# The 31-step inverse of the triangular blocks on GpSimd instead of VectorE, in a GLA + RWKV-7 layer on one Trainium2 core

## The chip, the cores and the metric

One core of a Trainium2 chip runs the whole layer. The metric is device time in microseconds (us), the median over several runs of the kernel; less is better. Beside the times there is one profiled execution with its trace. Engine names in the profile: PE is TensorE (PEld its weight loads), DVE is VectorE, ACT is ScalarE, POOL is GpSimd, SP is SyncE, which issues all DMAs of this kernel.

## What is computed

One inference step of a hybrid decoder layer, in float32, for a prompt of 1024 rows and 8 single-token samples, width 1024. A projection `w_in` (1024 to 9360 columns) feeds two branches and two gates:

```python
p = einsum('btd,dn->btn', x, w_in)                  # GLA, RWKV-7 and gate columns
S = diag(a_t) S + k_t^T v_t ;  o_t = q_t S          # GLA, 4 heads of 128 x 256
S = S (diag(w_t) - kk_t^T (kk_t * a_t)) + v_t^T k_t # RWKV-7, 16 heads of 64 x 64
y_t = S r_t
m = sigmoid(gate_a) * (o_gla @ w_up_gla) + sigmoid(gate_b) * (o_rwkv @ w_up_rwkv)
y = layernorm(2**0.25 * x + m @ w_out)
```

The outputs are `y`, the new states of both branches and the last projected row. The RWKV-7 recurrence is the part that matters here. In chunks of 64 tokens it becomes matrix products, if for each chunk and head the inverse of a unit triangular 64 x 64 matrix is at hand.

## The kernel before

**Stages.** The prompt is worked in two passes of 512 tokens (`PASS`; the samples ride with the first). In both passes TensorE computes `w_in` by rows of 128 columns, every product as three fp32r products of high and low halves (`blocks`, lines 670 to 705). While these run, each finished group of rows feeds a stream of its own: four GLA heads (`gla_head`) and eight pairs of RWKV heads (`pair`) in each pass, so 16 pairs in all. Then come the two up projections, and last `w_out` with the layer norm.

**A pair** runs `front`, `back`, `turn`, `chain` and `norm`. `front` (line 1060) computes decays and keys, then for its eight chunks the products `big<-az,wide`, masked into the tile `gg` (lines 1125 to 1130). The diagonal 32 x 32 blocks of these are written to DRAM (`LD`) and read back (`wide<-LD`, lines 1137 to 1145) so that 128 partitions hold 128 entries of work: 32 blocks, each four times, eight columns of the inverse for each partition. Lines 1147 to 1152 form the inverse by substitution: 31 steps, each a `tensor_mul` into the tile `Xt` and a `tensor_add` of it into the tile `X`. Every one of the 62 instructions reads what the one ahead of it wrote. Step j handles `ni = j // 4 + 1` rows of `w = 31 - j` elements, 8 to 76 elements for each partition. Then `X` goes to DRAM (`XD`) and back in another layout (`XT<-XD`), and `back` (line 1179) begins: `Xt<-XT` transposes on VectorE, then the products `big<-Xt,L` on TensorE which complete the 64 x 64 inverse. `chain` runs the eight chunks of the recurrence one after the other; pair p's chain waits for that of pair p - 1. There is one `X`, one `Xt`, one `L1`, and buffers for two pairs.

**What sets the order.** All engines run instructions in the order in which the program gives them, and a planner in the kernel (class `Order`, lines 239 to 402) writes that order. Each stream yields one instruction at a time; `run` takes the one with the smallest key (its start by the planner's own clock, less a priority). The start comes from `start`: when the engine is free, when the inputs are ready (plus a hop between engines, 0.13 for the same engine), and, for VectorE and GpSimd instructions that `shared` names (two SBUF inputs and the like), when the other of the two engines has left the shared port. `price` (lines 145 to 174) gives each instruction's cost. Instructions made through `self.E` may go to VectorE or GpSimd, whichever ends first by that clock, those through `self.C` to ScalarE or VectorE. So a change of engine or of price moves instructions everywhere. Every instruction is recorded through one helper, so that the profile shows line 217 for all; the tiles tell them apart.

The lines that the diff touches are 171 (in `price`) and 1150 and 1152 (in `front`).

## Time and profile before

| | |
|---|---|
| median of 3 runs | 1603.45 us (1600.87 to 1605.56) |
| profiled execution | 1597.82 us, span 1596.0 us |
| PE busy / PEld busy | 1550.1 us (97%) / 1371.0 us (86%) |
| DVE busy | 1282.5 us (80%), 3351 instructions |
| ACT busy | 855.9 us (54%) |
| POOL busy | 123.5 us (8%), 218 instructions |
| granted TensorE clock | 0.997 |

How to read it: busy time is the sum of an engine's instructions, the span runs from the first to the last instruction. Matmuls are pipelined and their ends are modelled, so PE's busy time also covers short holes between them. A group's row in the profile gives the engine, the operation, the tile written and the tiles read, the shape of output and input, the count, then busy time in us and the mean of one in ns, then the idle time of the engine ahead of them and what ended it. In the views of stretches, each engine has its busy time with the number of instructions in brackets.

### The profile page before, as it was taken

What the parts mean: (1) busy time and instruction counts of PE and PEld (TensorE: products, weight loads), DVE (VectorE), ACT (ScalarE), POOL (GpSimd) and SP (SyncE); (2) the same over time, 40 slices, a digit from 0 to 9 for tenths busy, and PEclk for the clock granted to TensorE, in tenths of its full rate; (3) what the DMA queues carried; (4) which work ended last, traced back from release to release, by engine and by line L of the source; (5) the groups of instructions that cost most, each with busy time, mean ns of one, the idle gap of its engine ahead of it and who ended that gap; (6) DMA issues with size and microseconds to landing.
All of it is one profiled execution on the core that took longest, in us unless ns stands there. A gap on an engine that the chain in (4) does not pass through costs nothing.

```text
span 1596.0 us, 29099 instructions
## 1 busy us (share of the span) xinstructions
PE 1550.1 (97%) x9874; PEld 1371.0 (86%) x9874; DVE 1282.5 (80%) x3351; ACT 855.9 (54%) x2032; POOL 123.5 (8%) x218
## 2 busy tenths in 40 slices
PE   8999999999999999999999999999999999999998
PEld 6999999999999998787888777878777889988786
DVE  6697889878989798779788997899877786756565
ACT  5564666566657665553654464445454646544210
POOL 2011001100000011001101120011001000000000
PEclk9999999999999999999999999999999999999999
DMA  9767776676757765755465546544665467797332
GB/s 308 245 233 221 231 232 224 204 260 222 232 188 250 246 219 184 213 162 172 144 194 161 168 119 212 168 152 134 204 174 144 161 211 255 255 300 251 128 117 82
DMA packets 206641, 318.42 MB, mean 200 GB/s; under 512 B 87076, under 2 KB 102573, under 8 KB 206493
## 3 DMA queue, kind: packets, MB, share of 16 engines
q1 hardware_dynamic: 206492, 316.56, 62.6%
q8 instruction: 79, 1.29, 0.3%
q14 instruction: 70, 0.57, 0.1%
HBM read 196.82 MB, written 118.61 MB: 198 GB/s over the span
## 4 chain that ended last, share of the span: by engine, by line
PE 60%; DVE 23%; DMA 6%; SPq 4%; issue 4%; ACT 3%; POOL 0%; DVEq 0%; POOLq 0%; ACTq 0%
PE proj L217 30%; PE big L217 19%; DVE row L217 8%; PE pY L217 7%; PE pch L217 4%; SPq L217 4%; DVE Xt L217 3%; DVE X L217 3%; DVE wide L217 2%; DVE wpart L217 2%; DMA wide<-LD 1%; DVE az L217 1%; DMA wraw<-w_in 1%; ACT row L217 1%; DVE pair L217 1%
## 5 line engine op out<-in xcount | busy, mean ns | idle before, releaser
L217 PE MATMUL proj<-xh,wpart 128*128 128x256 f32 (+2 forms) x3744 | 915.5, 328 | 2.4 <-DMA wpart<-w 2.0
L217 PEld LDWEIGHTS proj<-xh,wpart 128*128 128x128 f32 x3744 | 624.2, 189 | 52.3 <-issue 5.1
L217 PE MATMUL proj<-xl,wpart 128*128 128x264 f32 (+2 forms) x1872 | 611.6, 327 | 0.9 <-DVE xl L217 0.7
L217 PEld LDWEIGHTS proj<-xl,wpart 128*128 128x128 f32 x1872 | 353.3, 189 | 25.4 <-issue 1.7
L217 ACT CAST wpart<-wraw 128x512 fp32r<-128x512 f32 x210 | 130.3, 623 | 113.7 <-PE proj L217 44.0
L217 DVE TENSOR_TENSOR wpart<-wraw,wpart 128x512 fp32r<-128x512 f32 x207 | 142.3, 689 | 38.1 <-ACT wpart L217 37.3
L217 DVE TENSOR_TENSOR row<-row 128x512 f32<-128x512 f32 (+10 forms) x302 | 164.0, 549 | 7.3 <-ACT row L217 2.4
L217 ACT ACTIVATE row<-row 128x512 f32<-128x512 f32 (+5 forms) x229 | 139.1, 611 | 36.0 <-DVE row L217 25.2
L217 DVE TENSOR_TENSOR Xt<-X,wide 128x60 f32<-128x60 f32 (+24 forms) x496 | 108.7, 219 | 17.9 <-DMA wide<-LD 6.8
L217 DVE TENSOR_TENSOR X<-X,Xt 128x60 f32<-128x60 f32 (+24 forms) x496 | 109.0, 220 | 12.3 <-DVE Xt L217 0.5
L217 ACT ACTIVATE s0p<-wide,pc 64x64 f32<-64x64 f32 x256 | 88.0, 344 | 46.7 <-DVE wide L217 41.0
L217 POOL TENSOR_TENSOR row<-row 128x256 f32<-128x256 f32 (+5 forms) x67 | 67.2, 1005 | 575.8 <-DVE row L217 238.6
L217 ACT ACTIVATE row<-proj,omu 128x256 f32<-128x256 f32 (+1 forms) x99 | 54.1, 547 | 98.6 <-PE proj L217 98.4
L217 PE MATMUL big<-row 128*128 128x128 f32 (+3 forms) x520 | 96.4, 287 | 9.4 <-DVE Xt L217 4.0
L217 PEld LDWEIGHTS big<-row 128*128 128x128 f32 (+1 forms) x520 | 74.8, 187 | 20.0 <-ACT row L217 11.3
L384 ACT ACT_TABLE_LOAD x66 | 84.7, 1283 | 1.1
L217 DVE SCALAR_TENSOR_TENSOR wide<-pch,pc,s0p 64x64 f32<-64x64 f32 x224 | 63.2, 282 | 22.7 <-PE pch L217 17.4
L217 DVE SCALAR_TENSOR_TENSOR row<-proj,pv,row 128x255 f32<-128x255 f32 (+1 forms) x99 | 56.2, 568 | 26.6 <-ACT tail L217 17.5
L217 PE MATMUL big<-xh,wpart 128*128 128x512 f32 (+2 forms) x304 | 74.8, 329 | 0.0
L217 ACT COPY row<-big 128x128 f32<-128x128 f32 (+5 forms) x134 | 38.5, 317 | 64.8 <-PE big L217 56.5
L217 PE MATMUL big<-az,wide 128*128 128x256 f32 x256 | 66.4, 384 | 0.4 <-DVE row L217 0.2
L217 PE MATMUL big<-part,headsr 128*128 128x512 f32 x128 | 55.7, 440 | 7.3 <-ACT part L217 3.4
(240 smaller groups left out, 2506.9 us busy)
## 6 DMA issues: line engine op xcount, KB each, us to landing
w<-wpart SPq DMA_DIRECT2D x146, 512.0 KB
wpart<-w SPq DMA_DIRECT2D x146, 512.0 KB
wraw<-w_in SPq DMA_DIRECT2D x146, 256.0 KB
wide<-LD SPq DMA_DIRECT2D x64, 128.0 KB
wraw<-w_up_gla SPq DMA_DIRECT2D x32, 256.0 KB
wraw<-w_up_rwkv SPq DMA_DIRECT2D x32, 256.0 KB
sg<-row SPq DMA_DIRECT2D x16, 260.0 KB
row<-sg SPq DMA_DIRECT2D x16, 260.0 KB
```

What stands on the lines that cost most here:

```text
L217: ways.append((eng, lambda call=call: call(out, *args, **kw), price(eng, name, out, args, ins)))
L384: self.nc.scalar.preload_act_table_set(self.table)
```

## The change

Both instructions of each of the 31 steps are issued on GpSimd (`self.G`) instead of VectorE (`V`). Nothing else of the pair is altered: the memsets of `X` stay with `self.E`, the DMAs on SP. A second edit is in the planner: a `copy_predicated` on VectorE is priced at 480 elements a microsecond instead of 960. It issues no other instruction, but takes part in the order.

```diff
@@ price @@
         scalars = sum(x.free_size() == 1 for x in ins[1:]) if name in ("scalar_tensor_tensor", "tensor_scalar") else 0
-        return 0.068 + wide / 960 + 0.06 * scalars
+        return 0.068 + wide / (480 if name == "copy_predicated" else 960) + 0.06 * scalars
     if name in ("tensor_scalar", "memset"):
         return 0.08 + n / 760
     return 0.1 + n / (300 if name == "tensor_copy" else 456)
@@ front @@
         for j in range(31):
             w, ni = 31 - j, j // 4 + 1
             tv = tm[:, :ni * w].rearrange("p (s t) -> p s t", t=w)
-            yield V.tensor_mul(tv, X[:, 0:ni, j:j + 1].to_broadcast([P, ni, w]),
+            yield self.G.tensor_mul(tv, X[:, 0:ni, j:j + 1].to_broadcast([P, ni, w]),
                                L[:, j:j + 1, j + 1:].to_broadcast([P, ni, w]))
-            yield V.tensor_add(X[:, 0:ni, j + 1:], X[:, 0:ni, j + 1:], tv)
+            yield self.G.tensor_add(X[:, 0:ni, j + 1:], X[:, 0:ni, j + 1:], tv)
         self.free(tm)
```

## The prediction, made before the changed kernel was run

> **What bounds the kernel now.** First the page: busy shares, the chain of work that ended last, and the two groups that the change moves (busy us, mean ns of one, idle time ahead of them).

> ```profile
> PE 1550.1 (97%) x9874; PEld 1371.0 (86%) x9874; DVE 1282.5 (80%) x3351; ACT 855.9 (54%) x2032; POOL 123.5 (8%) x218
> ...
> PE 60%; DVE 23%; DMA 6%; SPq 4%; issue 4%; ACT 3%; POOL 0%; DVEq 0%; POOLq 0%; ACTq 0%
> ...
> L217 DVE TENSOR_TENSOR Xt<-X,wide 128x60 f32<-128x60 f32 (+24 forms) x496 | 108.7, 219 | 17.9 <-DMA wide<-LD 6.8
> L217 DVE TENSOR_TENSOR X<-X,Xt 128x60 f32<-128x60 f32 (+24 forms) x496 | 109.0, 220 | 12.3 <-DVE Xt L217 0.5
> ```

> TensorE is the bound: 97% busy, 60% of the chain. VectorE is second with 23% of the chain; GpSimd is empty. All TensorE idle time together is 1596.0 - 1550.1 = 46 us, the most that taking other engines out of its way is likely to win. Next, one stretch that holds the projection with the pairs, then the 16 stretches in which an inverse is formed (first `Xt` to last `X`; first, last and sum of 16), and the tile X alone in the same stretches. Columns: us, then each engine's busy time.

> ```profile
> 100.00:1300.00 1200.00, 1169.82 (x7552) 1039.79 (x7551) 1028.99 (x2855) 692.62 (x1692) 111.65 (x197) 1.00 0.62 193
> ```

> ```profile
> 77.00:114.40 37.40, 36.91 (x300) 36.34 (x299) 36.42 (x126) 20.30 (x49) 4.24 (x6) 1.00 0.73 253
> ...
> 1271.90:1298.10 26.20, 23.46 (x140) 20.84 (x139) 23.82 (x84) 13.90 (x25) 0.00 (x0) 0.93 0.79 275
> sum 475.40, PE 464.35 PEld 418.26 DVE 435.75 ACT 238.17 POOL 24.40; mean PE 29.02 PEld 26.14 DVE 27.23 ACT 14.89 POOL 1.53
> ```

> ```profile
> sum 475.40, DVE 217.47 POOL 0.00; mean DVE 13.59 POOL 0.00
> ```

> The order of the columns is PE, PEld, DVE, ACT, POOL. An inverse now takes 475.4 / 16 = 29.7 us, of which its own instructions are 13.6; the rest is other VectorE work between its steps. VectorE is 92% busy there (435.75 of 475.4) and 86% in the whole stage (1029 of 1200). TensorE loses only 11 us in these stretches: the projection covers the inverse. Third, what TensorE's queue waits for (sum, times, longest):

> ```profile
> PEld big L217 <- ACT row L217: 14.7, 20, 2.2
> PEld big L217 <- issue: 10.4, 16, 4.5
> PEld pch L217 <- DVE rh L217: 9.2, 20, 1.5
> PEld proj L217 <- issue: 6.8, 9, 0.9
> PEld big L217 <- DVE part L217: 5.7, 13, 1.3
> PEld big L217 <- ACT part L217: 5.1, 5, 2.7
> PEld big L217 <- DVE Xt L217: 3.9, 7, 1.3
> ```

> Many short waits. Over all 33 rows of that view, of which these are the first by size, those ended by VectorE sum to 31 us, those by ScalarE to 26. They are what a lighter VectorE can shorten.

> **What goes from VectorE.** 496 x 0.219 + 496 x 0.220 = 217.7 us. In the built program VectorE has 1026 instructions fewer (992 of the inverse, 34 others that the planner places elsewhere); POOL has 992 more and 22 besides. Table loads on ScalarE fall from 66 to 56:

> ```profile
> L384 ACT ACT_TABLE_LOAD x66 | 84.7, 1283 | 1.1
> ```

> ```profile
> L217 DVE COPY_PREDICATED row<-lev,big 128x256 f32<-128x256 uint8 x40 | 29.5, 737 | 1.1 <-PE big L217 0.8
> ```

> That is 10 x 1.28 = 12.8 us of ScalarE, which at 54% has room: I count nothing for it (bounds 0 to -5 us). The new price of `copy_predicated`, 0.068 + 256/480 = 0.60, is nearer to 0.737 than the old 0.33; it only makes the order truer, and I count nothing for it either (-5 to +5 us, as any reshuffling).

> **What a step costs on POOL.** The trace has no POOL instruction of 8 to 76 elements in these forms, so it is bounded by neighbours: groups by form, then one tile's minimum / median / maximum, then the timeline (start, us) and a stretch with two instructions back to back.

> ```profile
> L217 POOL TENSOR_TENSOR row<-row 128x256 f32<-128x256 f32 x29 | 24.3, 839 | 277.8 <-DVE row L217 96.3 <-PE big L217 96.0 <-DVE Xt L217 50.6
> L217 POOL TENSOR_TENSOR row<-row 128x8 f32<-128x8 f32 x4 | 1.1, 283 | 5.0 <-DVE row L217 4.9
> L217 POOL TENSOR_TENSOR row<-row 128x32 f32<-128x32 f32 x1 | 0.2, 240 | 10.4 <-issue 10.4
> L217 DVE TENSOR_TENSOR wpart<-wraw,wpart 128x512 fp32r<-128x512 f32 x207 | 142.3, 689 | 38.1 <-ACT wpart L217 37.3
> ```

> ```profile
> L217 POOL TENSOR_TENSOR row<-row x67: 203/1007/1925, 92.8 to 1258.4; 128x256 f32<-128x256 f32 x29, 128x512 f32<-128x512 f32 x22, 128x520 f32<-128x520 f32 x6, 128x8 f32<-128x8 f32 x4
> L217 POOL TENSOR_TENSOR part<-row,part x12: 1284/1327/1808, 268.7 to 1205.2; 128x512 fp32r<-128x512 f32 x12
> ```

> ```profile
> 263.80 0.63 POOL L217 TENSOR_TENSOR row<-row 128x256 f32<-128x256 f32 x1 [10.47 <-DVE row L217]
> ```

> ```profile
> 459.25:460.17 0.92, 0.84 (x2) 1.00 0.19 76
> ```

> The 31 products have sum(ni x w) = 1560 elements, 50.3 on the mean. Between 32 elements (0.240) and 256 undisturbed (0.63) the slope is 1.74 ns, so 50.3 elements take 0.272 us; 0.08 us lies between two neighbours (0.92 - 0.84). A step of 0.352 x 62 = **21.8 us** for an inverse that nothing disturbs. From below: 0.203 + 0.08, 17.5 us. From above: the mean rows, waits included, 0.283 at 8 and 0.839 at 256 elements, give 0.376 + 0.08, 28.3 us; and POOL against VectorE at 512 elements, 1284 / 689 = 1.86, times 0.2195 gives 0.409 + 0.08, 30.3 us. I take 21.8, since 32 elements is by far the nearest row.

> **The port.** POOL and VectorE hold each other up. VectorE alone, and POOL in the same stretch; then a POOL instruction behind a VectorE one:

> ```profile
> 494.29 0.22 DVE L217 TENSOR_TENSOR Xt<-X,wide 128x54 f32<-128x54 f32 x1
> 494.43 0.48 DVE L217 SCALAR_TENSOR_TENSOR row<-row 128x256 f32<-128x256 f32 x1
> 494.82 1.30 DVE L217 TENSOR_TENSOR X<-X,Xt 128x54 f32<-128x54 f32 x1
> ```

> ```profile
> 494.56 1.49 POOL L217 TENSOR_TENSOR part<-row,part 128x512 fp32r<-128x512 f32 x1 [32.36 <-ACT part L217]
> ```

> ```profile
> 758.84 0.68 DVE L217 TENSOR_TENSOR part<-row,part 128x512 fp32r<-128x512 f32 x1
> ...
> 759.07 0.52 POOL L217 TENSOR_TENSOR row<-row 128x4 f32<-128x4 f32 x1 [0.96 <-DVE row L217]
> ```

> `X` of 54 elements took 1.30 instead of 0.22 and ended with POOL's; POOL's 4 elements took 0.52 instead of 0.203, to 0.07 after VectorE's end. The other VectorE work in the stretches is 435.75 - 217.47 = 218.3 us in 475.4, a share of 0.46; I put half of it at instructions with two SBUF inputs (estimate from the groups; 0.3 to 0.7). In 25 us that is 5.8 us, some 8 instructions of 0.69, each holding a POOL step for about 0.5: **4.2 us** (2.5 to 6). VectorE in turn loses at most 8 x 0.27 x 16 = 35 us of its 218. The inverse then takes 21.8 + 4.2 = **26.0 us**, less than today's 29.7.

> **What of it shows.** TensorE executes in order: the products `big<-Xt,L` wait for the inverse, and everything behind them (projection, chain) waits with them. The planner has moved them: in the built program 292 TensorE instructions stand between the last `big<-az,wide` and the first `big<-Xt,L` of a pair on the mean, 320 before (368 for 429 in the first pass, 217 for 211 in the second). At 1200 us for 7552 records, 0.159 us (an f32 product leaves two records, so this is the least), 28 fewer are 4.4 us less cover, so an inverse of 29.7 - 4.4 = 25.3 us is just in time. Lateness: 0.7 us x 16 = **+11 us**. POOL's queue is in order too: behind a step stand low halves (`part`, `wpart`) and `row` products for TensorE. Most have had tens of us of idle time ahead of them, so a step of 0.35 matters little; cost nothing, bound +5 us. The four `XD<-X` DMAs stay in SP's queue and start when the last add ends, on another engine; no cost.

> Relief: VectorE in the stage falls from 1029 to about 1029 - 204 + 35 = 860 of 1200 us (15 of the 16 inverses), 86% to 72%; its idle share doubles, so I halve the 31 us of waits that it ends, and take a quarter off ScalarE's 26, which often stand behind VectorE: **-22 us** (0 to -46).

> Sum: 1597.8 + 11 - 22 = 1587 against the profiled execution, which lies 0.35% under the runs' median; on the median's scale **1592 us**, 0.7% faster.

> **Rivals.**

> (A) The step is priced by the mean rows, 0.456 us, and an inverse takes 28.3 us: 3.0 us late each, +48 - 22 = +26, **1629 us**, slower. It decides in the same place, the first `big<-Xt,L`, from an inverse of about 26.7 us on, where 16 latenesses of 1.4 eat the 22 us. For it: the means hold the port's waits that a busy VectorE causes. Against: 203, 240 and 0.63 are undisturbed.

> (B) POOL keeps its factor of 1.86 over VectorE on short instructions: 30.3 + 4.2 = 34.5 us, 9.2 late, 16 x 9.2 - 22 = +125, about **1728 us**. Against it: the fixed part would have to be 0.3 us, and 203 ns rows exist. [...]

> (C) TensorE is the bound anyway and lateness and relief cancel: 1598 to 1608, **1603 us**. For it: TensorE's 97%. That the move does not take place at all is excluded by the built order.

> **How the numbers follow.** Forecast 0.50, A 0.24, B 0.12, C 0.14. About 0.3% (4.8 us) is what a measurement here can tell from no change. The forecast's own spread, 1570 to 1600, lies almost wholly under 1598.6: faster 0.50. C gives same 0.14; A and B slower 0.36. Low end 1565: nearly all 46 us of TensorE's idle time gone. High end 1650: A with the larger port share (6 us for 4.2, 16 x 1.8 = 29 us, partly). Outside lie B and some 0.07 of tails.

> **What would show it.** Right: POOL busy from 123 to about 420 us (992 x 0.272 + 147), VectorE about 1050 to 1100, inverses near 26 us, waits of PEld for `rh`, `part` and `row` shrinking, that for `Xt` about 10 us more. Wrong: POOL's `X` rows at 0.35 us or more, inverses over 27 us and a long wait of TensorE for `Xt` (A, B); or inverses in time and PE's waits unchanged (C). If VectorE's rows of two SBUF inputs grow by much more than 35 us together, the port is what I undervalued.

## The result, and the profile after

| | before | after |
|---|---|---|
| median of 4 runs | 1603.93 us (1600.87 to 1605.56) | 1615.63 us (1614.06 to 1619.66) |
| profiled execution, span | 1596.0 us | 1617.9 us |
| TensorE idle (span less PE busy) | 45.9 us | 59.2 us |
| granted TensorE clock | 0.997 | 0.985 |

The ratio is **1.0079** [1.0055, 1.0103]: 0.8% slower, where 0.7% faster was forecast. The page of after, with its busy shares, its slices of the granted clock, its chain, the two groups of the inverse and the table loads:

```profile
PE 1558.7 (96%) x9874; PEld 1385.2 (86%) x9874; DVE 1110.1 (69%) x2325; ACT 846.4 (52%) x2034; POOL 479.2 (30%) x1232
...
PEclk9999999999999999999989999899999999999999
...
PE 75%; DVE 9%; POOL 5%; DMA 4%; issue 3%; ACT 2%; SPq 1%; POOLq 0%; DVEq 0%; ACTq 0%
...
L217 POOL TENSOR_TENSOR Xt<-X,wide 128x60 f32<-128x60 f32 (+24 forms) x496 | 168.6, 340 | 395.1 <-DMA wide<-LD 186.4
...
L217 POOL TENSOR_TENSOR X<-X,Xt 128x60 f32<-128x60 f32 (+24 forms) x496 | 167.5, 338 | 38.5
...
L384 ACT ACT_TABLE_LOAD x56 | 71.8, 1283 | 1.0
```

Almost everything that the change was to do has happened. VectorE fell from 80% to 69% of the span and from 23% to 9% of the chain; the 992 instructions stand on POOL at 0.34 us each, with 38.5 / 496 = 0.08 us ahead of an add. What is new is in the second row: two slices of 40 us in the second half of the span with less than 0.9 of the clock (before has a mean clock of 0.997).

The same stretches as before (us, then PE, PEld, DVE, ACT, POOL, granted clock, DMA share, GB/s): the projection, then the 16 inverses, first, last and sum.

```profile
100.00:1300.00 1200.00, 1158.03 (x7418) 1035.42 (x7417) 850.42 (x1855) 672.61 (x1671) 426.08 (x1107) 0.98 0.59 189
```

```profile
77.30:105.40 28.10, 28.10 (x232) 27.93 (x232) 21.16 (x48) 12.82 (x34) 23.29 (x63) 1.00 0.89 301
...
1298.00:1326.40 28.40, 27.38 (x184) 24.69 (x184) 14.59 (x23) 12.58 (x22) 23.62 (x62) 1.00 0.69 229
sum 416.40, PE 412.62 PEld 372.07 DVE 237.53 ACT 206.66 POOL 340.45; mean PE 25.79 PEld 23.25 DVE 14.85 ACT 12.92 POOL 21.28
```

An inverse takes 416.4 / 16 = 26.0 us, 3.7 less than before. VectorE is busy for 237.53 of these 416.4 us, 57% instead of 92%, and TensorE loses 416.4 - 412.6 = 3.8 us while they run. The inverse is not what got slower. What the weight loads of TensorE's queue wait for:

```profile
PEld big L217 <- issue: 16.2, 19, 4.9
PEld proj L217 <- issue: 12.9, 10, 5.6
PEld proj L217 <- DMA wpart<-w: 7.6, 2, 5.7
...
PEld pch L217 <- DVE rh L217: 4.4, 8, 1.4
PEld big L217 <- ACT row L217: 3.5, 7, 0.9
```

Over all rows of this view the waits ended by VectorE sum to 23.2 us (31 before) and those ended by ScalarE to 13.2 (26 before): 21 us less, where 22 was forecast. But others took their place: issue 33.7 (19.6), DMAs 10.0 (5.7), POOL 6.7 (0.2). Two things stand in the trace that the prediction has no term for.

**Holes.** A hole is measured here, and below where nothing else is said, from the start of TensorE's last product ahead of it to the start of the next one; the idle time in it is some 0.3 to 0.8 us shorter. The matmuls' own queue waits for projection weights, first before, then after (us, times, longest):

```profile
PE proj L217 <- DMA wpart<-w: 2.0, 2, 1.8
```

```profile
PE proj L217 <- DMA wpart<-w: 12.1, 3, 5.3
```

One of the two longest of these holes (5.57 us; the other, at 1177.3, has 5.67), on the timeline of TensorE and of SP's queue in after (start, us):

```profile
1012.21 0.40 PE L217 MATMUL proj<-xh,wpart 128*128 128x512 f32 x1
1017.78 0.76 PE L217 MATMUL proj<-xh,wpart 128*128 128x512 f32 x1 [5.18 <-DMA wpart<-w]
1020.82 1.06 PE L217 MATMUL big<-Xt,L 128*128 128x32 f32 x4 [2.27 <-DVE Xt L217]
```

```profile
997.83 4.03 SPq L217 DMA_DIRECT2D wpart<-w  x2
1005.32 2.67 SPq L217 DMA_DIRECT2D XD<-X  x4
1008.04 2.56 SPq L217 DMA_DIRECT2D L<-gg  x4
1010.76 2.92 SPq L217 DMA_DIRECT2D XT<-XD  x6
1013.78 2.05 SPq L217 DMA_DIRECT2D wpart<-w  x4
```

SP waits from 1001.9 to 1005.3 for the last add of the inverse, then issues 14 DMAs of the pair, `XD`, `L1` (which the view calls `L`) and `XT`, and only at 1013.78 the next weights. TensorE is idle for 5.18 us, runs one product, and is idle again.

The second stop is ahead of `big<-Xt,L`, the place at which the prediction had looked for lateness. All of TensorE's idle time ahead of these products, before and then after:

```profile
L217 PE MATMUL big<-Xt,L 128*128 128x32 f32 x128 | 16.6, 271 | 2.4 <-DVE Xt L217 1.7 <-ACT wpart L217 0.6
```

```profile
L217 PE MATMUL big<-Xt,L 128*128 128x32 f32 x128 | 19.1, 292 | 9.3 <-issue 6.6 <-DVE Xt L217 2.5 <-PE proj L217 0.2
```

It is 6.9 us more. Most of it bears the name "issue" and so doesn't show in the waits for `Xt`. The largest of these holes, 4.70 us idle up to 843.07, is the inverse all the same: SP issues its `XT<-XD` until 837.95, and VectorE's transposes `Xt<-XT` run from 841.73 to 842.97.

**Half clock.** The first product behind the hole took 0.76 us, the same product ahead of it 0.40. Stretches of after with the granted clock at 0.50: the three longest, and the sum of all eight.

```profile
841.24:851.48 10.24, 7.26 (x31) 6.46 (x32) 9.36 (x21) 3.58 (x11) 0.00 (x0) 0.50 0.10 41
1015.32:1025.56 10.24, 5.50 (x16) 4.45 (x17) 7.85 (x12) 1.02 (x4) 5.74 (x9) 0.50 0.52 194
189.30:196.10 6.80, 6.80 (x32) 6.70 (x32) 4.22 (x7) 4.12 (x9) 0.00 (x0) 0.50 0.97 355
...
sum 44.38, PE 36.30 PEld 32.16 DVE 30.85 ACT 16.27 POOL 6.68; mean PE 4.54 PEld 4.02 DVE 3.86 ACT 2.03 POOL 0.83
```

Before had one such stretch of 3.4 us. (Every kernel of this study has one more at its very end, which is left out here and below.) The lengths are 3.4, 6.8 and 10.2 us, multiples of 3.41, and the two longest begin some 3 us after the start of a hole: the one at 841.2 after a hole of 4.98 us that began at 838.1, the one at 1015.3 after that of the timeline above, at 1012.2.

**Where 21.9 us come from.** In after neighbouring products of 128x512 start 0.43 us apart at half clock (1023.97, 1024.40, 1024.83) and 0.23 at full (1009.67, 1009.90), those of 128x256 0.21 and 0.12 (medians): 1.8 times. As an estimate I take twice, as the granted 0.50 has it, so that half of PE's busy time in those stretches is loss; by 1.8 times the 18.2 us of after would be some 16. Between the two spans: TensorE idle +13.3 us (ahead of the products `proj<-xh,wpart`, which wait for weights, 13.4 instead of 2.4, +11.0; ahead of `big<-Xt,L` +6.9; all others together -4.6); half of its busy time at half clock 18.2 instead of 1.7, +16.5; what remains, 1540.5 instead of 1548.4, -7.9. Relief is real, and holes with their half clock take more than it gives.

### The profile page after: what moved, and what is told of

Its sections match the earlier page's. It is cut to its first block, busy times and chain, and to the rows that moved or that the text cites. A ratio compares the mean times of both kernels' runs of the same rounds, so it can differ in the third digit from the quotient of the medians.

```text
span 1617.9 us, 29035 instructions
## 1 busy us (share of the span) xinstructions
PE 1558.7 (96%) x9874; PEld 1385.2 (86%) x9874; DVE 1110.1 (69%) x2325; ACT 846.4 (52%) x2034; POOL 479.2 (30%) x1232
## 4 chain that ended last, share of the span: by engine, by line
PE 75%; DVE 9%; POOL 5%; DMA 4%; issue 3%; ACT 2%; SPq 1%; POOLq 0%; DVEq 0%; ACTq 0%
PE proj L217 42%; PE big L217 21%; PE pY L217 8%; PE pch L217 4%; DVE row L217 4%; POOL X L217 2%; POOL Xt L217 2%; DVE wide L217 1%; SPq L217 1%; DVE az L217 1%; ACT row L217 1%; DMA row<-sg 1%; DVE wpart L217 1%; DMA wide<-LD 1%; DMA wpart<-w 1%
## 5 line engine op out<-in xcount | busy, mean ns | idle before, releaser
L217 PE MATMUL proj<-xh,wpart 128*128 128x256 f32 (+2 forms) x3728 | 915.9, 330 | 13.4 <-DMA wpart<-w 12.1
L217 PEld LDWEIGHTS proj<-xh,wpart 128*128 128x128 f32 x3728 | 626.1, 190 | 66.5 <-issue 11.1
L217 PE MATMUL proj<-xl,wpart 128*128 128x264 f32 (+2 forms) x1864 | 612.6, 329 | 0.0
L217 PEld LDWEIGHTS proj<-xl,wpart 128*128 128x128 f32 x1864 | 355.2, 191 | 23.5 <-issue 1.7
L217 POOL TENSOR_TENSOR Xt<-X,wide 128x60 f32<-128x60 f32 (+24 forms) x496 | 168.6, 340 | 395.1 <-DMA wide<-LD 186.4
L217 ACT CAST wpart<-wraw 128x512 fp32r<-128x512 f32 x210 | 130.1, 623 | 114.7 <-PE proj L217 53.3
L217 DVE TENSOR_TENSOR wpart<-wraw,wpart 128x512 fp32r<-128x512 f32 x203 | 141.6, 699 | 62.8 <-ACT wpart L217 61.4
L217 POOL TENSOR_TENSOR X<-X,Xt 128x60 f32<-128x60 f32 (+24 forms) x496 | 167.5, 338 | 38.5
L217 POOL TENSOR_TENSOR row<-row 128x256 f32<-128x256 f32 (+6 forms) x90 | 87.1, 972 | 278.9 <-DVE row L217 148.8
L217 DVE TENSOR_TENSOR row<-row 128x256 f32<-128x256 f32 (+7 forms) x279 | 151.9, 556 | 13.6 <-DMA row<-state_rwkv 6.0
L217 ACT ACTIVATE row<-row 128x512 f32<-128x512 f32 (+4 forms) x229 | 138.7, 611 | 37.9 <-DVE row L217 23.3
L217 ACT ACTIVATE row<-proj,omu 128x256 f32<-128x256 f32 (+1 forms) x99 | 54.1, 547 | 113.9 <-PE proj L217 103.9
L217 DVE SCALAR_TENSOR_TENSOR row<-proj,pv,row 128x255 f32<-128x255 f32 (+1 forms) x99 | 56.5, 571 | 81.1 <-ACT tail L217 55.0
L217 ACT ACTIVATE s0p<-wide,pc 64x64 f32<-64x64 f32 x256 | 88.0, 344 | 40.5 <-DVE wide L217 31.2
L217 PE MATMUL big<-row 128*128 128x128 f32 (+3 forms) x520 | 96.9, 287 | 2.8 <-POOL row L217 1.4
L217 DVE SCALAR_TENSOR_TENSOR wide<-pch,pc,s0p 64x64 f32<-64x64 f32 x224 | 63.1, 282 | 40.4 <-PE pch L217 36.1
L217 PEld LDWEIGHTS big<-row 128*128 128x128 f32 (+1 forms) x520 | 76.0, 189 | 9.8 <-POOL row L217 1.9
L217 PE MATMUL big<-xh,wpart 128*128 128x512 f32 (+2 forms) x320 | 79.3, 330 | 0.4 <-ACT xh L217 0.4
L217 POOL TENSOR_SCALAR XT<-XT,st 128x256 f32<-128x256 f32 x1 | 1.2, 1231 | 258.8 <-ACT st L217 258.8
L384 ACT ACT_TABLE_LOAD x56 | 71.8, 1283 | 1.0
L217 ACT COPY row<-big 128x384 f32<-128x384 f32 (+5 forms) x131 | 37.4, 316 | 56.9 <-PE big L217 55.7
L217 PE MATMUL big<-az,wide 128*128 128x256 f32 x256 | 64.5, 383 | 0.8 <-DVE gg L217 0.4
```

The source lines that it names most:

```text
L217: ways.append((eng, lambda call=call: call(out, *args, **kw), price(eng, name, out, args, ins)))
L384: self.nc.scalar.preload_act_table_set(self.table)
```

## Experiments

Two theories at first. **PLACE**, which the expectations call POOL: the move to GpSimd itself costs time here (a late inverse, GpSimd's queue, holes behind the DMAs that follow it). **ORDER**: the planner's order, which both edits reshuffle, decides, and the engine of the inverse little. Every ratio is against before on the same chip; lower is faster. TensorE's idle time, half clock and remainder of all profiled runs stand in one table further down.

### One edit at a time

`e1_pool_only` keeps the move and takes back the price; `e2_price_only` does the reverse.

```diff
 # e1_pool_only: after, with
-        return 0.068 + wide / (480 if name == "copy_predicated" else 960) + 0.06 * scalars
+        return 0.068 + wide / (960 if name == "copy_predicated" else 960) + 0.06 * scalars
 # e2_price_only: after, with
-            yield self.G.tensor_mul(tv, ...
+            yield V.tensor_mul(tv, ...
-            yield self.G.tensor_add(X[:, 0:ni, j + 1:], X[:, 0:ni, j + 1:], tv)
+            yield V.tensor_add(X[:, 0:ni, j + 1:], X[:, 0:ni, j + 1:], tv)
```

> The changed kernel without its price edit: the inverse on POOL, copy_predicated at 960 again. Two theories. ORDER: the inverse on POOL costs nothing by itself (it takes 26.0 us there, as forecast); the loss is that this combination of prices made the planner write an order of instructions with long holes of TensorE, and another order has fewer. POOL: the engine itself costs it: the inverse ends late behind the port, XD<-X blocks SP's queue with the weights behind it, TensorE has holes of 2 to 6 us and runs at half clock after them. ORDER expects 1590 to 1607 us here and less than 15 us at half clock; POOL expects 1611 to 1625 us and some 45 us at half clock, as in the changed kernel.

> The kernel before with the price edit alone: copy_predicated at 480, the inverse on VectorE. ORDER and POOL both expect about the time before, 1595 to 1611 us (ORDER a little wider than POOL, since any price writes another order). A third theory, PRICE, says that the truer price of copy_predicated is what costs the time: it expects 1611 to 1625 us here.

Measured: e1 1590.16 us, 0.9918 [0.9892, 0.9944]; e2 1608.04 us, 1.0032 [1.0015, 1.0049]. The move alone gains 0.8%, within 2 us of the forecast of 1592. The price alone costs 0.3%. Together they cost 0.8%: on top of the move the price edit is worth 1.0079 / 0.9918, +1.6%. PRICE, which put the loss on the price edit by itself and expected 1611 us or more of e2, falls; PLACE as the only cause falls with e1, which it had at 1611 or more. The page of e1:

```profile
PE 1546.1 (97%) x9874; PEld 1370.9 (86%) x9874; DVE 1116.6 (70%) x2369; ACT 852.5 (54%) x2033; POOL 454.0 (29%) x1193
```

VectorE and POOL have about the loads that they have in after, and still the two kernels lie 25 us apart. The edit between them issues no instruction; it changes the order, and with it the engine of some 40 instructions that the planner may place (VectorE 2369 for 2325, POOL 1193 for 1232). In what follows, an order means both.

### Other prices

If the order decides, then any other price of `copy_predicated` should throw the time about, on either engine.

```diff
 # e3_price_500, e7_pool_560: after, with 500 or 560 for 480
 # e6_dve_500, e10_dve_560: the same, and the inverse back on V
-        return 0.068 + wide / (480 if name == "copy_predicated" else 960) + 0.06 * scalars
+        return 0.068 + wide / (500 if name == "copy_predicated" else 960) + 0.06 * scalars
```

> The changed kernel with copy_predicated at 500 instead of 480, which changes 0.601 to 0.580 us for one kind of instruction in the planner, and so the order, but no mechanism. ORDER expects a visibly different time, 1590 to 1608 us; POOL and PRICE expect the changed kernel's 1611 to 1620 us.

> The kernel before (inverse on VectorE) with copy_predicated at 500: the partner of the kernel with 500 and the inverse on POOL, which took 1595.0 us. The theory as it stands: POOL saves VectorE some 200 us and with it about 10 us of TensorE's waits, whatever the order, and each order adds its own holes, worth 0 to 25 us. It expects 1598 to 1612 us here, above the POOL partner. The rival, that the engine makes no difference and only orders do, expects 1590 to 1612 us, above or below the partner alike.

> The changed kernel with copy_predicated at 560: one more order with the inverse on POOL. The theory (POOL saves about 10 us, orders scatter) expects 1588 to 1602 us, with under 30 us at half clock; the rival (POOL itself costs time and 1590 and 1595 were the lucky ones) expects 1605 us or more.

> The kernel before with copy_predicated at 560, partner of the 560 kernel on POOL (0.14% faster than before). So far POOL against VectorE in three pairs of equal prices: 0.8% faster (960), 0.5% slower (480), 0.7% slower (500). If the engine decides nothing and the order everything, any time from 1583 to 1610 us can come, and the mean of the four differences lies within 0.4% of zero. If POOL saves about 10 us on the mean, this one takes 1604 us or more.

e3 took 1595.01 us, as ORDER had it. e7, at 1599.72 us, still fitted a GpSimd that saves some 10 us; e6 and e10, at 1582.76 and 1595.04 us, where 1598 and 1604 or more were expected of that theory, do not.

| price (elements a us) | VectorE | GpSimd | GpSimd against VectorE |
|---|---|---|---|
| 960 | 1 (before) | 0.9918 [0.9892, 0.9944] (e1) | -0.8% |
| 480 | 1.0032 [1.0015, 1.0049] (e2) | 1.0079 [1.0055, 1.0103] (after) | +0.5% |
| 500 | 0.9883 [0.9861, 0.9906] (e6) | 0.9948 [0.9931, 0.9964] (e3) | +0.7% |
| 560 | 0.9955 [0.994, 0.9969] (e10) | 0.9986 [0.9969, 1.0002] (e7) | +0.3% |

At 500 instead of 480, a price that differs by 0.02 us for an instruction of 256 elements, GpSimd's kernel is 1.3% and VectorE's 1.5% faster. From best to worst the orders spread over 1.6% (GpSimd) and 1.5% (VectorE); the four differences between the engines have both signs and a mean of +0.15%. So e1's gain is not the worth of the move: it is one draw of four. With 500 and the inverse on VectorE, e6 took **1582.76 us**, the fastest kernel of the study and faster than both that were given. Its page:

```profile
PE 1543.9 (98%) x9874; PEld 1368.6 (87%) x9874; DVE 1282.8 (81%) x3351; ACT 840.5 (53%) x2006; POOL 138.1 (9%) x236
```

VectorE does as much work here as before (1282.5 us). What is different is TensorE: 36.6 us idle, no hole over 2.31 us behind the start (where every kernel waits some 4.5 us for its first data), no half clock but the one at the end.

### Order and engine apart

The planner writes the order for the engine that it sees. These two keep one kernel's order and issue the inverse on the other engine.

```diff
 # e4_before_order_pool: before, with
+        self.I = Engine(V=nc.gpsimd)
-            yield V.tensor_mul(tv, ...              # and the tensor_add
+            yield self.I.tensor_mul(tv, ...
 # e9_after_order_dve: after, with
+        self.I = Engine(G=nc.vector)
-            yield self.G.tensor_mul(tv, ...         # and the tensor_add
+            yield self.I.tensor_mul(tv, ...
```

> The order of the kernel before, kept instruction by instruction (the planner still counts the inverse on VectorE), but its 992 instructions are issued on POOL. So the engine changes and the order does not. ORDER expects that VectorE is relieved and nothing else happens: inverses of 22 to 27 us, below the 29.7 that this order allows, and 1585 to 1604 us. POOL expects late inverses, holes and half clock: 1610 us or more.

> The changed kernel's order kept, instruction by instruction, with the 992 instructions of the inverse issued on VectorE. With the swap in the order of before (POOL there: 0.4% slower) it completes a square of two engines and two orders. If the changed kernel loses because of its order, whatever the engine, the time stays near its own, 1609 to 1622 us; above 1622 if VectorE in addition can't do 26 us inverses (the order allows no more) beside its other work. If POOL itself is what costs, the time falls to 1590 to 1608 us.

| | inverse on VectorE | on GpSimd |
|---|---|---|
| order of before | 1 | 1.0043 [1.0024, 1.0062] (e4, 1609.76 us) |
| order of after | 1.0146 [1.0123, 1.0168] (e9, 1625.31 us) | 1.0079 [1.0055, 1.0103] |

The order of after is slow on either engine, by 1.46% on VectorE and 0.36% on GpSimd (1.0079 / 1.0043). But ORDER alone does not hold either: it had e4 at 1604 or less, with inverses of 22 to 27 us, and they took 28.5. In e9, on VectorE, they took 26.7 us for the 26.0 of after, and 1625.31 us lies above the 1622 that was expected if VectorE can't do its inverses in time. Lateness is not what the trace of e9 shows, though: TensorE is idle ahead of `big<-Xt,L` for 7.2 us there, 9.3 in after, and less at half clock too; what is larger in e9 is the remainder in the table below, by 10.4 us. Each order fares best on the engine that it was written for. In e4 the reason can be read: TensorE's waits for GpSimd, then a place on TensorE's and on POOL's timeline.

```profile
PE big L217 <- POOL part L217: 9.4, 3, 4.2
```

```profile
969.98 0.40 PE L217 MATMUL proj<-xh,wpart 128*128 128x512 f32 x1
...
974.62 0.80 PE L217 MATMUL big<-part,headsr 128*128 128x512 f32 x1 [4.24 <-POOL part L217]
```

```profile
973.07 0.28 POOL L217 TENSOR_TENSOR Xt<-X,wide 128x48 f32<-128x48 f32 x1
973.31 1.26 POOL L217 TENSOR_TENSOR part<-row,part 128x512 fp32r<-128x512 f32 x1
974.52 0.28 POOL L217 TENSOR_TENSOR X<-X,Xt 128x48 f32<-128x48 f32 x1
```

A low half (`part`) that TensorE needs stands in POOL's queue behind steps of an inverse, because the order was written when POOL was empty at that time. TensorE waits 4.24 us for it and goes on at half clock (0.80 us for a product of the shape that took 0.40). `e8_before_order_lo_dve` takes those low halves out of POOL's queue:

```diff
 # e4, and in addition
+        self.L = Engine(V=nc.vector, G=nc.vector)
-        yield (self.V if x.space == PSUM else self.E).tensor_sub(lo, x, hi.bitcast(F32))
+        yield (self.V if x.space == PSUM else self.L).tensor_sub(lo, x, hi.bitcast(F32))
```

> The order of before with the inverse on POOL, which took 1609.8 us and had 9.4 us of TensorE's time waiting for low halves (part) of POOL, which stood between steps of the inverse. Here those of the low halves that the planner gave to POOL are issued on VectorE at their place in the order; all else is kept. If the queue behind the inverse is what kept the swap of engines from paying: those waits go, half clock falls from 37 us to under 25, and the time to 1590 to 1602 us. If not, it stays at 1606 to 1613 us.

Measured: 1605.19 us, 1.0017 [1.0001, 1.0033], between the two expectations. The waits for POOL's `part` are gone, and 0.26 of the 0.43% with them (the two intervals overlap), but TensorE now waits for VectorE in their place:

```profile
PE big L217 <- DVE part L217: 6.6, 8, 3.8
PE big L217 <- DVE Xt L217: 6.2, 5, 4.1
```

In both runs the inverse is also late: TensorE's idle time ahead of `big<-Xt,L` is 9.0 us in e4 and 11.1 in e8, where before has 2.4.

### The DMAs behind the inverse

In after the weights stand behind 14 DMAs of the pair in SP's queue. If that is the price of the late inverse, issuing the 14 elsewhere should give it back.

```diff
 # e5_end_dmas_pool: after, with Engine(S=nc.gpsimd); e11_end_dmas_act: with Engine(S=nc.scalar)
+        self.Q = Engine(S=nc.gpsimd)
-            yield self.S.dma_start(XD.rearrange(...)[q], X[NU * q:NU * q + NU])   # and L1, XT
+            yield self.Q.dma_start(XD.rearrange(...)[q], X[NU * q:NU * q + NU])
```

> The changed kernel in its own order, but the 14 DMAs that follow each inverse (four to XD, four into L1, six out of XD) are issued from POOL's queue, where the last add has just run, instead of SP's, where the second pass's weights (wpart<-w) stand behind them. If SP's queue is how the changed kernel loses time: TensorE's wait for wpart<-w falls from 12.1 us to under 5, time at half clock from 44 us to 30 or less, and the time to 1598 to 1609 us. If the holes have other causes, the time stays at 1612 to 1620 us. It may be slower still (over 1620) if POOL needs much longer to issue a DMA than SP's 0.6 us, since `back` waits for these.

> The changed kernel's order, with the 14 DMAs that follow each inverse issued from ScalarE's queue instead of SP's (from POOL's queue they made it 4% slower, with TensorE waiting for POOL's other work). If SP's queue is where the second pass's weights are held up, TensorE's wait for wpart<-w falls from 12.1 us to under 5 and the half clock stretches that follow those two holes (10.2 and 3.4 us) go; the time falls to 1596 to 1611 us, unless ScalarE, held up by the wait for the inverse, opens other holes: then the wait for wpart<-w still falls, and waits for ACT rise. If the weights are late for another reason, their wait stays above 8 us.

Measured: e5 1669.95 us, 1.042 [1.0391, 1.045]; e11 1651.39 us, 1.0303 [1.0275, 1.0331]. In both the wait for `wpart<-w` is gone from TensorE's waits, and others are larger than it was, first e5, then e11:

```profile
PE big L217 <- POOL row L217: 19.3, 8, 5.4
PE big L217 <- POOL part L217: 13.8, 5, 3.8
PE big L217 <- DVE Xt L217: 9.3, 2, 7.6
```

```profile
PE big L217 <- DVE Xt L217: 14.2, 3, 6.9
PE big L217 <- ACT row L217: 11.5, 8, 2.3
```

Everything behind the 14 in the new queue is late instead, and from the end of `X` to the first `big<-Xt,L` it takes 16.7 us (e5) and 16.3 (e11) for 14.2 in after. POOL's queue issued one of the 14 in 0.58 us in e5, no slower than SP's in after (8.15 us for the 14 of the timeline above, 0.58 each), so the issuing itself is not what e5 loses by. So SP's queue does cause the weights' hole, but neither run shows what after would take without it.

### What a hole costs

`e12_holes` puts five holes of chosen length into the last stage of e6, where TensorE is otherwise all but gapless (busy for 18.00 of 18.00 us from 1482 to 1500 in e12, and for 21.87 of 22.00 from 1506 to 1528): before a block of `w_out`, a chain of 2, 5, 9, 14 or 20 `tensor_add` on a tile of its own, then a transpose of it on TensorE. It adds work and leaves none out.

```diff
 # e6, and before five blocks of the last stage
+                    yield self.V.tensor_copy(self.hole[:m], q[:, :P])
+                    for _ in range(steps):
+                        yield self.V.tensor_add(self.hole[:m], self.hole[:m], self.hole[:m])
+                    pt = yield from self.bank("pch", [P, m])
+                    yield self.tr(pt, self.hole[:m])
```

> The fastest kernel so far (inverse on VectorE, 500; no half clock before the end) with five holes of TensorE made on purpose in the last stage, where it otherwise issues without a stop: ahead of five groups of products it waits for a chain of 2, 5, 9, 14 and 20 small VectorE instructions, some 1, 2, 3, 5 and 7 us. They are extra work that changes no output. If holes are what halves the clock, the granted clock falls to 0.5 behind the long ones (from 3 to 5 us on) and not behind the first, in stretches of 3.4 us or a multiple; each then costs its length and half of what TensorE does in the stretch. If the half clock in the changed kernel came from something else (load, POOL), no stretch follows these holes.

Measured in one execution only: 1610.17 us, span 1608.4 against 1580.5 for e6. The five transposes, with the idle time ahead of them, then TensorE's busy time and granted clock in the stretches at half clock and in one between them:

```profile
1480.62 0.33 PE L218 MATMUL pch<-cons,hole 128*128 128x128 f32 x1 [1.04 <-DVE hole L218]
1505.28 0.30 PE L218 MATMUL pch<-cons,hole 128*128 128x128 f32 x1 [2.11 <-DVE hole L218]
1531.28 0.30 PE L218 MATMUL pch<-cons,hole 128*128 128x128 f32 x1 [3.41 <-DVE hole L218]
1560.48 0.45 PE L218 MATMUL pch<-cons,hole 128*128 128x128 f32 x1 [5.05 <-DVE hole L218]
1581.42 0.45 PE L218 MATMUL pch<-cons,hole 128*128 128x128 f32 x1 [7.01 <-DVE hole L218]
```

```profile
1531.80:1535.20 3.40, 3.40 (x10) 0.50 0.54 187
1559.10:1565.90 6.80, 5.42 (x14) 0.50 0.01 3
1579.60:1586.40 6.80, 4.98 (x13) 0.50 0.01 2
1535.30:1555.00 19.70, 19.70 (x86) 1.00 0.20 68
```

From start to start the holes are 1.43, 2.50, 3.81, 5.44 and 7.40 us. Behind the first two the clock is whole (1.00 from 1482 to 1500 and from 1506 to 1528); the other three are followed by one or two stretches of 3.41 us at half clock (3.40, 6.80 and 6.80 above). Between such stretches the clock is whole (1.00 from 1535.3 to 1555.0). The sum used above holds here: idle 55.7 - 36.6 = 19.1, half of 3.40 + 5.42 + 4.98 = 6.9, together 26.0 of the 27.9 us by which the span grew. By that sum each hole of 3.8 to 7.4 us cost 1.7 to 2.7 us more than itself.

Between these lengths it mattered in the traces where a hole lies. In each run all stretches at half clock begin on one grid of 3.413 us (in after to within 0.01 us, from 189.29 on), and the grid lies elsewhere in each execution. Cut along it, behind the start, the 14 traces show this: behind all 70 steps in which TensorE was idle for 1.93 us or more the next step was at half clock, and behind none of the 6131 steps at full clock with less than 0.7 us idle; of the steps at full clock in between it was 22 of 221. A hole of 2.76 us in before was split by the grid and left the clock whole; one of 2.59 us in after lay within one step and was followed by half clock. Here are the two steps of before and the one of after (us, TensorE's busy time, granted clock, DMA share, GB/s):

```profile
123.24:126.66 3.42, 2.04 (x17) 1.00 0.93 236
126.66:130.07 3.41, 2.32 (x12) 1.00 1.03 331
```

```profile
1121.13:1124.55 3.42, 1.10 (x9) 1.00 0.37 131
```

### All profiled runs by one sum

| | span | TensorE idle | at half clock | half of PE's busy time in it | remainder |
|---|---|---|---|---|---|
| before | 1596.0 | 45.9 | 3.4 | 1.7 | 1548.4 |
| e2, price 480, VectorE | 1605.9 | 52.9 | 10.2 | 5.1 | 1547.9 |
| e6, 500, VectorE | 1580.5 | 36.6 | 0 | 0 | 1543.9 |
| e10, 560, VectorE | 1590.0 | 44.0 | 3.4 | 1.7 | 1544.2 |
| e9, order of after, VectorE | 1620.8 | 59.2 | 27.3 | 10.7 | 1550.9 |
| after, 480, GpSimd | 1617.9 | 59.2 | 44.4 | 18.2 | 1540.5 |
| e1, 960, GpSimd | 1589.1 | 42.9 | 10.2 | 3.6 | 1542.5 |
| e3, 500, GpSimd | 1592.6 | 42.0 | 27.3 | 12.1 | 1538.5 |
| e7, 560, GpSimd | 1597.3 | 45.9 | 17.1 | 8.4 | 1543.0 |
| e4, order of before, GpSimd | 1609.7 | 52.9 | 37.5 | 16.7 | 1540.1 |
| e8, e4 with low halves on VectorE | 1600.0 | 46.1 | 27.3 | 10.9 | 1543.0 |
| e5, DMAs from POOL | 1658.5 | 89.0 | 71.7 | 29.3 | 1540.2 |
| e11, DMAs from ScalarE | 1651.2 | 79.2 | 71.7 | 28.9 | 1543.0 |

Spans lie 78 us apart, remainders 12. The five kernels with the inverse on VectorE have a mean remainder of 1547.1, the eight on GpSimd 1541.4: 5.7 us less, outside of TensorE's visible idle time, which I put down to the lighter VectorE; no run tests that by itself. The four orders written for GpSimd (after, e1, e3, e7) lose 10.6 us to half clock on the mean, the four for VectorE (before, e2, e6, e10) 2.1, and that takes the 5.7 back (in single executions; the medians of the eight are the table of prices). Each of the four for GpSimd has a hole over 3 us in the second pass (5.67, 6.52, 4.26 and 3.25 us); none of the four for VectorE has one over 2.83.

## Why the prediction was wrong, step by step

The prediction's sum was +11 for lateness and -22 for relief. The trace has +6.9 for lateness, +11.0 for weights, +16.5 for half clock (by the estimate above), -4.6 for all other waits of TensorE and -7.9 outside of its idle time, together +21.9.

- **An inverse of 26.0 us**: right. 0.340 and 0.338 us for an instruction, port waits included, where 0.272 + 4.2 / 62 = 0.340 was worked out; 26.0 in after. The median instruction took 0.30, the mean of VectorE's was 0.2195, so POOL's factor on these short ones is 1.4, and 1.5 with port waits. Rivals A and B fall with it: B's 1.86 was measured at 512 elements, and that it holds at 50 was an estimate. POOL's busy time came to 479 for 420, since waits for the port lie inside its instructions and I had left them out of that sum: in after 145 of the 992 took over 0.1 us more than the median of their tile and shape, 53 us more in all, and 137 of the 145 ended within 0.2 us behind the end of a VectorE instruction (217 of the other 847). (The bound from the mean rows should read 0.378 us for 0.376; nothing hangs on it.)
- **VectorE's loss at the port** (35 us at most): its forms that remain grew by some 13 us in all. That it is busy for 850 us in the stage where 860 was worked out is in part luck: VectorE's records of neighbouring instructions overlap (taken one by one they sum to 1406.9 us in before, 124.4 more than the busy time, and to 1186.7 in after, 76.6 more), so its whole busy time fell by 172 us (1282.5 to 1110.1) and not by 217.7, and the loss at the port was put too high.
- **Relief of 22 us**: its sum came out, 21 us less of those waits, but by luck. I had halved VectorE's 31 us and taken a quarter off ScalarE's 26; VectorE's fell by a quarter (7.8 us) and ScalarE's by half (12.8). Wrong as to what follows from it: other waits rose by as much, and outside of TensorE's idle time relief came to 5.7 us on the mean of the orders, 7.9 here.
- **Lateness of 11 us at `big<-Xt,L`**: the place is right and the size near it, 6.9 us more idle time; the form is not. It is not 0.7 us for each of 16 pairs but three holes with 4.70, 2.27 and 1.90 us idle. In e1, e3 and e7, with the inverse on GpSimd too, TensorE is idle there for 1.3 to 1.4 us in all, so this loss also belongs to the order. An inverse in time by the mean says nothing of the one that is not, and the few long holes carry the loss.
- **The price edit at nothing, "-5 to +5 us, as any reshuffling"**: this is the step that failed. The same edit is +0.3% on VectorE (e2) and +1.6% on top of the move (25 us), and 500 for 480 takes 1.3% back. Over four prices the orders of this kernel spread by 1.5 to 1.6%, some 25 us: more than the effect that was to be forecast, and five times my bound. That e1, the move without the price, came within 2 us of the forecast is luck for the same reason.
- **A hole costed once**: the second failure. No term had the clock; 16.5 of the 21.9 us are it by the sum. The five holes of e12 part between 2.50 and 3.81 us, but the length of a hole alone does not tell: in after the stretches at 189.3, 499.9, 578.4 and 1124.5 follow holes of 1.62, 1.43, 2.17 and 2.59 us, while one of 2.76 in before is followed by none. What the 14 traces show is that 1.93 us of idle time in one step of the grid were followed by half clock in all 70 cases, and less at times, from one hole or several together.
- **The `XD` DMAs in SP's queue at no cost**: wrong in after; with ten more behind them they delay weights by 8.5 us, and the wait for `wpart<-w` rose from 2.0 to 12.1 us.
- **Behind a step in POOL's queue, cost nothing, bound +5 us**: the bound is too low where the order does not allow for it (9.4 us in e4). In after, whose order does, the waits ended by POOL sum to 6.7, of which 4.6 are for `part` and `row`.
- **Rival C**, TensorE as the bound with relief and lateness cancelling, is nearest to what the mean of four orders shows (+0.15%), though by another route: relief against half clock.

What stays open: why every order written for GpSimd leaves TensorE longer holes in the second pass. The DMAs behind the inverse are one cause, shown in after; that they are the only one is not shown, since taking them off SP opened other holes. Nor do they make a long hole by themselves: before has the same row of them from 1136.31 us on, with the weights at 1145.15, and a hole of 2.24 us. The engine has a part in it: TensorE's wait for `wpart<-w` is 6.9 us in e9 and 12.1 in after, of one order, and 2.0 in before and 4.2 in e4, of the other. That half clock explains the spread of the times is argued from the sum, with e12 as its only direct test. And four orders for each engine are few: a difference of some tenths of a per cent between the engines could hide in them.

## What to carry to other kernels

Where a planner in the kernel writes the order, an edit is one new draw of the order: try it under several prices that should not matter, on both sides, before the edit gets credit or blame, and keep the best draw (here the old engine with another price, 1.2% faster than before). For an engine that bounds the kernel, count its holes by length and not only by sum, since here long ones of TensorE were paid a second time in the clock (behind 70 of 70 steps of 3.413 us with 1.93 us idle or more). Taking load off the second engine was worth what the first visibly waited for (21 us less of it), less the waits that came up behind those (25 us more of them: issue 33.7 for 19.6, DMAs 10.0 for 5.7, POOL 6.7 for 0.2).

## What the runs showed of the hardware

```profile
L217 POOL TENSOR_TENSOR Xt<-X,wide x496: 201/297/1736, 77.3 to 1325.5; 128x60 f32<-128x60 f32 x16, 128x28 f32<-128x28 f32 x12, 128x66 f32<-128x66 f32 x11, 128x48 f32<-128x48 f32 x10
```

- Which queue issued the 14 small DMAs of each pair mattered here: against SP, ScalarE's queue was 2.2% slower (1.0303 / 1.0079), GpSimd's 3.4% (1.042 / 1.0079).
